# SwiGLU FFN of a decoder layer: gate and upper products by Strassen block sums, in two phases

## The chip, the core and the metric

The kernel runs on one core of a Trainium2 chip. The metric is the device time of one execution in microseconds (us); less is better. TensorE (PE) multiplies matrices, VectorE (DVE), ScalarE (ACT) and GpSimd (POOL) do elementwise work, SyncE (SP) issues DMAs. Each engine takes its instructions in the order of its own queue, and waits there for the engines or DMAs whose results it needs.

## The reference

One layer of a decoder: a combined projection, three head groups (a gated chunk MLP and two attentions), an output projection, and a SwiGLU FFN. D is 1024, D_FF is 2816; there are 1024 prompt tokens and 64 sample rows, 1088 in all. Everything is float32.

```python
def norm(x, g):                                    # rms_norm in the source
    y = x * rsqrt(mean(x * x, axis=-1) + EPS)
    return y * g
def swiglu(x, w_in, w_out):                        # w_in: 1024 x 5632, w_out: 2816 x 1024
    h = x @ w_in
    return (jax.nn.silu(h[..., :D_FF]) * h[..., D_FF:]) @ w_out
# one layer, for the prompt (1024 rows) and for the samples (8 x 8 rows, with a paged cache)
u, va, qb, kb, vb, qc, kc, vc, lf = split_proj(rms_norm(yp, g_attn) @ w_in, b_f)
a_out = chunk_spatial_gate(u, rms_norm(va, g_v), w_s, b_s)
b_out = sb_prompt(qb, kb, vb)                      # stick-breaking attention, 6 heads
c_out = fox_prompt(qc, kc, vc, lf)                 # forgetting attention, 6 heads
yp = yp + merge_groups(a_out, b_out, c_out, g_mix, w_o)
yp = yp + swiglu(rms_norm(yp, g_ffn), w_ffn_in, w_ffn_out)
y_prompt = rms_norm(yp, g_final)
```

## The kernel before

The change is in the FFN, which is the end of the program. A float32 product is formed from three products of operands in the fp32r type: each operand is split into a high part (an ACT copy) and a low part (the rest, a DVE subtraction), and high x high, high x low and low x high are added up in the same PSUM bank (lines 1326 to 1328).

Ahead of the FFN, `merge` adds the output projection to `y`, one tile of 128 tokens and one half of 512 columns after the other (`prod`, L1147 to L1153; its weights `wor`, `woh`, `wol`). `step` (L1247) normalises a token tile that is complete (`norm`, `xs` at L196) and, `LAG` = 4 tiles later, transposes an earlier one on PE (`spread`, L204) and writes its high part by ACT (`xh`, L206) and its low part by DVE (`xl`, L207). When the merge is done the last four tiles are still to be spread; L1317 to L1319 do that between the first and the second chunk of tokens of the first pair.

`y` stays in SBUF for the whole FFN, as do `xh2` and `xl2`, the two parts of all tokens. The FFN goes over 22 pairs of column blocks: block `ff` of the gate and block `ff` of the upper matrix, 1024 x 128 each. Each is loaded (`fraw_`, L1308), split (`fh`, `fl`, L1311 and L1312), and multiplied by three chunks of tokens (384, 384, 320), with 8 steps along D (L1325). ACT takes the Silu of the gate, DVE multiplies it by the upper (L1332), ACT and POOL split the result g (`g_h` L1333, `g_l` L1335). After every `FCH` = 2 pairs the output product runs: 9 token tiles x 2 halves of 512 columns, three matmuls per block and tile (`fout`, L1359 to L1362; two for the samples' tile), added to `y` by DVE (L1363). After the last group each tile is normalised and written out (`final`, L1281).

PSUM has two sets of banks: `fgu` shares three (set a), `fout` and `spread` share five (set b). The order on each engine is made by a scheduler when the program is built; a matmul waits for a bank until its last reader is done. SP issues the DMAs in one queue, first in, first out.

## Time and profile before

| | us |
|---|---|
| median of 3 runs (lowest, highest) | 1645.32 (1643.71, 1648.43) |
| the profiled execution | 1652.82 |
| its span | 1651.1 |
| PE busy in it | 1559.6 |
| DVE, ACT, POOL busy | 862.3, 627.7, 474.7 |
| mean granted clock of TensorE, share of full speed | 0.976 |

A profile belongs to one execution. A matmul's shown duration is longer than the distance to the next one's start, since matmuls are pipelined; what a matmul costs in a row of them is read from the distance of the starts. In the names, `fgu<-xh,fh` is a matmul from `xh` (moving) and `fh` (weights) into the PSUM tile `fgu`; 128x384 is partitions by columns of the moving operand.

### The profile page before, as it was taken

To read this page: it belongs to the slowest core of one execution; us is meant where nothing else is said; L and a number is where in the kernel's file an instruction comes from. 1 tells how busy PE (TensorE), PEld (TensorE's weight loads), DVE (VectorE), ACT (ScalarE), POOL (GpSimd) and SP (SyncE) were. 2 spreads that over 40 slices of the span, in tenths; PEclk is the share of its full clock that TensorE was granted. 3 is DMA by queue.
4 is the path that set the end of the run, shared out by engine and by line. 5 is a ranking of instruction groups with operands and counts; after the bars stand their busy time and mean duration, and the time that the engine had idled before them with its cause. 6 is when DMAs were issued, how large, how long until landed. Compare 5 with 4: busy or idle time off the path is not lost.

```text
span 1651.1 us, 23878 instructions
## 1 busy us (share of the span) xinstructions
PE 1559.6 (94%) x8980; PEld 1439.6 (87%) x8980; DVE 862.3 (52%) x1565; ACT 627.7 (38%) x1291; POOL 474.7 (29%) x596
## 2 busy tenths in 40 slices
...
GB/s 174 56 168 180 187 187 147 114 134 236 222 204 227 234 182 165 290 175 127 88 83 84 39 38 52 44 45 41 52 52 26 52 51 42 36 52 51 26 1 108
DMA packets 137303, 184.54 MB, mean 112 GB/s; under 512 B 17844, under 2 KB 110372, under 8 KB 137188
## 3 DMA queue, kind: packets, MB, share of 16 engines
...
## 4 chain that ended last, share of the span: by engine, by line
PE 52%; DVE 2%; DMA 2%; issue 1%; POOL 0%; ACT 0%; SPq 0%; DVEq 0%; POOLq 0%; ACTq 0%
PE fgu L1326 11%; PE fgu L1328 11%; PE fgu L1327 11%; PE fout L1360 5%; PE fout L1359 5%; PE fout L1362 5%; PE prod L1147 1%; PE prod L1148 1%; DMA lr<-linv 1%; PE prod L1150 1%; DMA wor<-in_w_o_dram 0%; DVE fl L1294 0%; PE spread L204 0%; DVE vh L812 0%; DVE cr L1107 0%
## 5 line engine op out<-in xcount | busy, mean ns | idle before, releaser
L1328 PE MATMUL fgu<-xh,fl 128*128 128x384 f32 (+1 forms) x1056 | 345.9, 328 | 1.0 <-DVE fl L1312 1.0
L1326 PE MATMUL fgu<-xh,fh 128*128 128x384 f32 (+1 forms) x1056 | 345.4, 328 | 0.8 <-ACT xh L206 0.5
L1327 PE MATMUL fgu<-xl,fh 128*128 128x384 f32 (+1 forms) x1056 | 345.7, 327 | 0.0
L1335 POOL TENSOR_TENSOR g_l<-sl,g_h 128x384 fp32r<-128x384 f32 (+1 forms) x66 | 75.1, 1138 | 672.9 <-ACT g_h L1333 672.9
L1363 DVE TENSOR_TENSOR y<-fout,y 128x512 f32<-128x512 f32 x198 | 135.6, 690 | 127.9 <-PE fout L1362 115.9
L1326 PEld LDWEIGHTS fgu<-xh,fh 128*128 128x128 f32 x1056 | 198.1, 188 | 2.9 <-ACT xh L206 0.8
L1328 PEld LDWEIGHTS fgu<-xh,fl 128*128 128x128 f32 x1056 | 198.3, 188 | 2.2 <-DVE fl L1312 1.3
L1327 PEld LDWEIGHTS fgu<-xl,fh 128*128 128x128 f32 x1056 | 198.3, 188 | 0.7
L1332 DVE TENSOR_TENSOR sl<-fgu,sl 128x384 f32<-128x384 f32 (+1 forms) x66 | 35.3, 535 | 301.4 <-PE fgu L1328 301.4
L1360 PE MATMUL fout<-fol,g_h 128*128 128x512 f32 x396 | 156.6, 395 | 0.0
L1359 PE MATMUL fout<-foh,g_h 128*128 128x512 f32 x396 | 156.5, 395 | 0.0
L1362 PE MATMUL fout<-foh,g_l 128*128 128x512 f32 x352 | 139.1, 395 | 0.0
L812 POOL TENSOR_TENSOR vh<-vr,vh 128x384 fp32r<-128x384 f32 x96 | 102.4, 1083 | 80.0 <-ACT vh L811 59.7
L1333 ACT CAST g_h<-sl 128x384 fp32r<-128x384 f32 (+1 forms) x66 | 32.6, 493 | 184.6 <-DVE sl L1332 184.6
L743 PE MATMUL sqk<-kt,qz 128*128 128x512 f32 x288 | 99.3, 439 | 3.0 <-DVE ats L800 1.2
L286 PE MATMUL pqk<-xh,wh 128*128 128x384 f32 (+1 forms) x288 | 97.0, 337 | 1.2 <-DVE pvt L599 0.6
L287 PE MATMUL pqk<-xl,wh 128*128 128x384 f32 (+1 forms) x288 | 95.5, 333 | 0.0
L288 PE MATMUL pqk<-xh,wl 128*128 128x384 f32 (+1 forms) x288 | 94.8, 333 | 0.0
L1360 PEld LDWEIGHTS fout<-fol,g_h 128*128 128x128 f32 x396 | 74.3, 188 | 16.7
L1359 PEld LDWEIGHTS fout<-foh,g_h 128*128 128x128 f32 x396 | 74.3, 188 | 16.7
L582 PE MATMUL apv<-at,vv 128*128 128x256 f32 x432 | 76.2, 299 | 10.3 <-DVE hl L302 4.8
L572 DVE TENSOR_TENSOR at<-atr,at 128x512 fp32r<-128x512 f32 (+2 forms) x144 | 76.3, 543 | 16.1 <-ACT at L571 15.5
...
## 6 DMA issues: line engine op xcount, KB each, us to landing
...
```

The source lines that it names most:

```text
L286: T.matmul(pm[:, 0:n], lhsT=wh, rhs=xh[:, k, o], start=k == 0, stop=False)
L287: T.matmul(pm[:, 0:n], lhsT=wh, rhs=xl[:, k, o], start=False, stop=False)
L288: T.matmul(pm[:, 0:n], lhsT=wl, rhs=xh[:, k, o], start=False, stop=k == KT - 1)
L743: T.matmul(pz, lhsT=queries(p, a, si), rhs=kts[t][p][:, b], start=si == 0 and p == 0 and n_ == 0, stop=si == 1 and p == 2 and n_ == 2)
L812: (V if t >= 16 and j in VL else G).tensor_tensor(vh[:, 1], vrs[t][:, j], f(vh[:, 0]), op=OP.subtract)
L1326: T.matmul(pm[:, 0:n], lhsT=h_[:, k], rhs=xh2[:, k, o], start=k == 0, stop=False)
L1327: T.matmul(pm[:, 0:n], lhsT=h_[:, k], rhs=xl2[:, k, o], start=False, stop=False)
L1328: T.matmul(pm[:, 0:n], lhsT=l_[:, k], rhs=xh2[:, k, o], start=False, stop=k == KT - 1)
L1359: T.matmul(pm, lhsT=gh[q][:, o], rhs=wh2[q][:, hs], start=q == 0, stop=False)
L1360: T.matmul(pm, lhsT=gh[q][:, o], rhs=wl2[q][:, hs], start=False, stop=i == 8 and end)
L1362: T.matmul(pm, lhsT=gl[q][:, o], rhs=wh2[q][:, hs], start=False, stop=end)
L1363: V.tensor_tensor(y[:, i, hs], pm, y[:, i, hs], op=OP.add)
```

## The change

The FFN becomes two phases. In the first the gate and upper products of all 22 pairs are made and g is written to DRAM (`gs`); in the second g and the weights of the output product are read back, split, and multiplied. `y` is written to DRAM (`ysc`) ahead of the first phase and read back (`z0` to `z7`) ahead of the second. In the first phase the tokens stand in two halves of 544 (`HT`), each in chunks of 272, and D in two halves, as `XH[d half, token half]` and `XL`.

Pairs 0 and 1 are multiplied in the ordinary form (`ordinary`), 192 matmuls of 272 columns each. The pairs from `NO` = 2 on take the 2 x 2 block product (gate and upper by token halves, over the two halves of D) in Strassen's form after Winograd: seven products instead of eight, of sums of blocks. The four sums of the tokens are made once, while the ordinary pairs run (`sums_of_tokens`, `last_sum`). The four sums of the weights are made for each pair on POOL (`wsum`), all seven weight blocks are split (`split`), and the seven products are put together by DVE, POOL and ACT (`first`, `second`). Products 1, 2, 3 of the next pair go before products 6, 5, 7, 4 of this one; the first three use the bank set a (`fgu`), the others set b (`fgs`).

In the second phase block 0 forms a group by itself, with operands made near the end of the first phase (`ops0`), and the other 21 blocks form seven groups of three (`FCH` = 3).

```diff
-FCH = 2
+FCH = 3
+HT = NTOK // 2
+RAWB, WSB = 2, 8
+NO = 2
+         "fgu": "a", "fgs": "b", "spread": "b", ...
+    gs = [dr.tile([128, NTOK], F32, name=f"gs{j}") for j in range(NFF)]
+    ysc = [dr.tile([128, D], F32, name=f"ysc{i}") for i in range(8)]
...
+    XH, XL = {}, {}
+    for th, dh in ((0, 0), (0, 1), (1, 1), (1, 0)):
+        XH[dh, th] = fp.tile([128, 4, HT], F32R, name=f"xh{dh}{th}")
+        XL[dh, th] = fp.tile([128, 4, HT], F32R, name=f"xl{dh}{th}")
...
+            if i < 8:
+                S.dma_start(ysc[i], y[i])
-            spread(x2, rows(i), i, xh2, xl2)
+            spread_halves(x2, rows(i), i)
     for _ in mg:
         step(LAG)
     ends[0](xin)
-    whole(8)
     pmp.close()
+    while xn:
+        step(0)
+    pyy.close()
...
+    def wload(j):
+        raws[j] = []
+        for half in range(2):
+            c0 = half * DFF + j * 128
+            r = slot(half)
+            if half:
+                r = f(r)[:, 0:D].rearrange("p (k c) -> p k c", c=128)
+            S.dma_start(r, w_ffn_in[0, :, c0:c0 + 128].rearrange("(k p) c -> p k c", p=128))
+            raws[j].append(r)
+    def wsum(j):
+        ga_, up = raws[j]
+        g1, g2, u1, u2 = ga_[:, 0:4], ga_[:, 4:8], up[:, 0:4], up[:, 4:8]
+        s1, s2, s3, s4 = (wf.tile([128, 4, 128], F32, name=f"s{x}") for x in range(4))
+        G.tensor_tensor(s1, u1, u2, op=OP.add)
+        G.tensor_tensor(s2, s1, g1, op=OP.subtract)
+        G.tensor_tensor(s4, g2, s2, op=OP.subtract)
+        G.tensor_tensor(s3, g1, u1, op=OP.subtract)
+        sums[j] = {1: g1, 2: g2, 3: s4, 4: u2, 5: s1, 6: s2, 7: s3}
+    def split(j, q):
+        src = sums[j].pop(q)
+        x = wf.tile([128, 2, 4, 128], F32R, name="ws", bufs=WSB)
+        A.copy(x[:, 0], src)
+        V.tensor_tensor(x[:, 1], src, f(x[:, 0]), op=OP.subtract)
+        parts[j, q] = x
+    NP = ((0, HT // 2), (HT // 2, HT))
+    FIRST, SECOND = (1, 2, 3), (6, 5, 7, 4)
+    XB = {}
+    def product(j, q, c):
+        a, b = NP[c]
+        w, (hi, lo) = parts[j, q], XB[q]
+        pm = bank([128, 512], "fgu" if q in FIRST else "fgs")
+        for k in range(4):
+            T.matmul(pm[:, 0:b - a], lhsT=w[:, 0, k], rhs=hi[:, k, a:b], start=k == 0, stop=False)
+            T.matmul(pm[:, 0:b - a], lhsT=w[:, 0, k], rhs=lo[:, k, a:b], start=False, stop=False)
+            T.matmul(pm[:, 0:b - a], lhsT=w[:, 1, k], rhs=hi[:, k, a:b], start=False, stop=k == 3)
+        return pm[:, 0:b - a]
+    def temp(name, bufs):
+        return wf.tile([128, HT // 2], F32, name=name, bufs=bufs)
+    def first(j, q, c):
+        pm = product(j, q, c)
+        a, b = NP[c]
+        if q == 1:
+            if c == 0:
+                gts[j, 0] = wf.tile([128, HT], F32, name="ga", bufs=2)
+            p = held[j, c, 1] = temp("p1", 4)
+            A.copy(p, pm)
+        elif q == 2:
+            o = gts[j, 0][:, a:b]
+            V.tensor_tensor(o, pm, held[j, c, 1], op=OP.add)
+            A.activation(o, o, AF.Silu)
+        else:
+            p = held[j, c, 3] = temp("p3", 4)
+            A.copy(p, pm)
+    def second(j, q, c):
+        pm = product(j, q, c)
+        a, b = NP[c]
+        if q == 6:
+            u = held[j, c, "u2"] = temp("u2", 2)
+            V.tensor_tensor(u, pm, held.pop((j, c, 1)), op=OP.add)
+        elif q == 5:
+            t = temp("t", 3)
+            V.tensor_tensor(t, pm, held[j, c, "u2"], op=OP.add)
+            if c == 0:
+                gts[j, 1] = wf.tile([128, HT], F32, name="gb", bufs=1)
+            o = gts[j, 1][:, a:b]
+            G.tensor_tensor(o, t, held.pop((j, c, 3)), op=OP.add)
+            A.activation(o, o, AF.Silu)
+            held[j, c, 5] = pm
+        elif q == 7:
+            u = held[j, c, "u3"] = temp("u3", 2)
+            V.tensor_tensor(u, pm, held.pop((j, c, "u2")), op=OP.add)
+            t = temp("t", 3)
+            V.tensor_tensor(t, held.pop((j, c, 5)), u, op=OP.add)
+            o = gts[j, 1][:, a:b]
+            G.tensor_tensor(o, o, t, op=OP.mult)
+            if c == 1:
+                S.dma_start(gs[j][:, HT:], gts.pop((j, 1)))
+        else:
+            t = temp("t", 3)
+            V.tensor_tensor(t, pm, held.pop((j, c, "u3")), op=OP.add)
+            o = gts[j, 0][:, a:b]
+            G.tensor_tensor(o, o, t, op=OP.mult)
+            if c == 1:
+                S.dma_start(gs[j][:, 0:HT], gts.pop((j, 0)))
+    XB[1], XB[2], XB[3] = ((XH[x], XL[x]) for x in ((0, 0), (1, 0), (1, 1)))
...
+    def ordinary(j, th, c):
+        a, b = NP[c]
+        pms = []
+        for h in range(2):
+            pm = bank([128, 512], "fgu")
+            for dh in range(2):
+                w, hi, lo = parts[j, (h, dh)], XH[dh, th], XL[dh, th]
+                for k in range(4):
+                    T.matmul(pm[:, 0:b - a], lhsT=w[:, 0, k], rhs=hi[:, k, a:b], start=dh == 0 and k == 0, stop=False)
+                    T.matmul(pm[:, 0:b - a], lhsT=w[:, 0, k], rhs=lo[:, k, a:b], start=False, stop=False)
+                    T.matmul(pm[:, 0:b - a], lhsT=w[:, 1, k], rhs=hi[:, k, a:b], start=False, stop=dh == 1 and k == 3)
+            pms.append(pm[:, 0:b - a])
+        if c == 0:
+            gts[j, th] = wf.tile([128, HT], F32, name="ga", bufs=2)
+        o = gts[j, th][:, a:b]
+        A.activation(o, pms[0], AF.Silu)
+        V.tensor_tensor(o, pms[1], o, op=OP.mult)
+        if c == 1:
+            S.dma_start(gs[j][:, th * HT:th * HT + HT], gts.pop((j, th)))
+    def sums_of_tokens(c):
+        a, b = NP[c]
+        for k in range(4):
+            (h11, l11), (h12, l12), (h21, l21), (h22, l22) = (
+                (f(XH[x][:, k, a:b]), f(XL[x][:, k, a:b])) for x in ((0, 0), (0, 1), (1, 0), (1, 1)))
+            t1, t2, t4 = temp("p1", 4), temp("p3", 4), temp("t", 3)
+            V.tensor_tensor(t1, h12, h11, op=OP.subtract)
+            V.tensor_tensor(t1, t1, l12, op=OP.add)
+            V.tensor_tensor(t1, t1, l11, op=OP.subtract)
+            V.tensor_tensor(t2, h22, t1, op=OP.subtract)
+            V.tensor_tensor(t2, t2, l22, op=OP.add)
+            G.tensor_tensor(t4, h21, t2, op=OP.subtract)
+            G.tensor_tensor(t4, t4, l21, op=OP.add)
+            for q, t, e in ((6, t2, V), (5, t1, V), (4, t4, G)):
+                hi, lo = (x[:, k, a:b] for x in XB[q])
+                A.copy(hi, t)
+                e.tensor_tensor(lo, t, f(hi), op=OP.subtract)
+    def last_sum(c):
+        a, b = NP[c]
+        for k in range(4):
+            h22, l22 = f(XH[1, 1][:, k, a:b]), f(XL[1, 1][:, k, a:b])
+            hi, lo = XH[0, 1][:, k, a:b], XL[0, 1][:, k, a:b]
+            t3 = temp(("u2", "u3")[k % 2], 2)
+            V.tensor_tensor(t3, h22, f(hi), op=OP.subtract)
+            V.tensor_tensor(t3, t3, l22, op=OP.add)
+            V.tensor_tensor(t3, t3, f(lo), op=OP.subtract)
+            A.copy(hi, t3)
+            V.tensor_tensor(lo, t3, f(hi), op=OP.subtract)
+    wload(0)
+    quarters(0)
+    wload(1)
+    ordinary(0, 0, 0)
+    if xn:
+        step(0)
+    ordinary(0, 0, 1)
+    whole(8)
+    while whole_ or xn:
+        step(0)
+    pxin.close()
+    ft = pool(pfp, "ft", side="left")
+    for q in (6, 5, 4):
+        XB[q] = (ft.tile([128, 4, HT], F32R, name=f"th{q}"), ft.tile([128, 4, HT], F32R, name=f"tl{q}"))
+    XB[7] = (XH[0, 1], XL[0, 1])
+    quarters(1)
+    wload(2)
+    ordinary(0, 1, 0)
+    sums_of_tokens(0)
+    ordinary(0, 1, 1)
+    wload(3)
+    for th, c in ((0, 0), (0, 1)):
+        ordinary(1, th, c)
+    sums_of_tokens(1)
+    wsum(NO)
+    for q in FIRST:
+        split(NO, q)
+    for c in range(2):
+        ordinary(1, 1, c)
+    last_sum(0)
+    for c in range(2):
+        for q in FIRST:
+            first(NO, q, c)
+    last_sum(1)
+    for q in SECOND:
+        split(NO, q)
+    wsum(NO + 1)
+    for q in FIRST:
+        split(NO + 1, q)
+    wload(NO + 2)
+    for j in range(NO, NFF):
+        if j + 1 < NFF:
+            for q in FIRST:
+                for c in range(2):
+                    first(j + 1, q, c)
+            for q in SECOND:
+                split(j + 1, q)
+        if j + 2 < NFF:
+            wsum(j + 2)
+        for q in SECOND:
+            for c in range(2):
+                second(j, q, c)
+        del raws[j]
+        if j + 2 < NFF:
+            for q in FIRST:
+                split(j + 2, q)
+        if j + 3 < NFF:
+            wload(j + 3)
+        if j == NFF - 2:
+            graw, raw, g_h0 = f(slot(1))[:, 0:NTOK], slot(0).rearrange("p k c -> p (k c)"), slot(1)
+            S.dma_start(raw, w_ffn_out[0, 0:128, :])
+            S.dma_start(graw, gs[0])
+            h_, l_, g_l0 = (wf.tile([128, 2, 4, 128], F32R, name="ws", bufs=WSB).rearrange("p a k c -> p (a k c)")
+                            for _ in range(3))
+            A.copy(h_, raw)
+            V.tensor_tensor(l_, raw, f(h_), op=OP.subtract)
+            A.copy(g_h0[:, 0:NTOK], graw)
+            G.tensor_tensor(g_h0[:, NTOK:], graw[:, SP_:], f(g_h0[:, SP_:NTOK]), op=OP.subtract)
+            V.tensor_tensor(g_l0, graw[:, 0:SP_], f(g_h0[:, 0:SP_]), op=OP.subtract)
+            ops0 = (g_h0, g_l0, h_, l_)
...
+    for i in range(8):
+        S.dma_start(y[i], ysc[i])
...
+    def out_operands(ff):
+        po = fo2[(ff - 1) // FCH % 2]
+        raw = fo.tile([128, D], F32, name="wor2", bufs=3)
+        S.dma_start(raw, w_ffn_out[0, ff * 128:ff * 128 + 128, :])
+        graw = fo.tile([128, NTOK], F32, name="gr", bufs=3)
+        S.dma_start(graw, gs[ff])
+        h_ = po.tile([128, D], F32R, name="foh", bufs=FCH)
+        l_ = po.tile([128, D], F32R, name="fol", bufs=FCH)
+        A.copy(h_, raw)
+        (G if ff == 2 else V).tensor_tensor(l_, raw, f(h_), op=OP.subtract)
+        g_h = po.tile([128, NTOK + NS], F32R, name="g_h", bufs=FCH)
+        g_l = po.tile([128, SP_], F32R, name="g_l", bufs=FCH)
+        A.copy(g_h[:, 0:NTOK], graw)
+        G.tensor_tensor(g_h[:, NTOK:], graw[:, SP_:], f(g_h[:, SP_:NTOK]), op=OP.subtract)
+        (V if ff % 2 and ff > 3 else G).tensor_tensor(g_l, graw[:, 0:SP_], f(g_h[:, 0:SP_]), op=OP.subtract)
+        made[ff] = (g_h, g_l, h_, l_)
...
+    for f0, nf in [(0, 1)] + [(x, FCH) for x in range(1, NFF, FCH)]:
+        for ff in range(f0 or 1, f0 + nf if f0 > 1 else 1 + FCH if f0 == 0 else 1):
+            out_operands(ff)
...
+        gh, gl, wh2, wl2 = zip(*(made.pop(ff) for ff in range(f0, f0 + nf)))
         for i in (8, 0, 1, 2, 3, 4, 5, 6, 7):
```

**The order on DVE at the first weight split.** Before: `xl` is a low part of the tokens, `xs` a normalised tile, `fl` at L1312 the low part of the first weight block.

```order
L196 SCALAR_TENSOR_TENSOR xs_9742<-y,rs,gfb 128x1024
L1138 TENSOR_TENSOR wol<-wor,woh 128x512 x2
L1089 TENSOR_SCALAR rv<-stat 128x1
L207 TENSOR_TENSOR xl_9285<-spread,xh_9284 128x4x128
L137 TENSOR_SCALAR ss<-ss 128x1
L207 TENSOR_TENSOR xl_9285<-spread,xh_9284 128x4x128
L1312 TENSOR_TENSOR fl<-fraw__9928,fh 128x1024
L1153 SCALAR_TENSOR_TENSOR y<-prod,fraw,y 128x512
L207 TENSOR_TENSOR xl_9285<-spread,xh_9284 128x4x128
```

After: `ws` at L1330 is the low part of the first weight block; `p` and `u` at L1436 and L1454 are sums of tokens in the making.

```order
L1454 TENSOR_TENSOR u_10727<-xh_9329,xh_9331 128x272
L1270 TENSOR_TENSOR xl_9332<-spread,xh_9331 128x4x128
L1270 TENSOR_TENSOR xl_9330<-spread,xh_9329 128x4x128
L1436 TENSOR_TENSOR p_10295<-p_10295,xl_9332 128x272
L1436 TENSOR_TENSOR p_10311<-p_10311,xl_9332 128x272
L1436 TENSOR_TENSOR p_10327<-p_10327,xl_9332 128x272
L140 TENSOR_SCALAR ss<-ss 64x1
L1436 TENSOR_TENSOR p_10343<-p_10343,xl_9332 128x272
L1330 TENSOR_TENSOR ws<-raw_10065,ws 128x512
```

The first split stood between two low parts of the tokens, with twelve more to come behind it; it now stands behind all spreads of the prompt's tiles and the first twelve operations of the sums.

**The order on DVE while the first pair is multiplied.** Before: `sl` at L1332 reads the PSUM bank of a chunk; it stands among the splits of weights.

```order
L1312 TENSOR_TENSOR fl<-fraw__10227,fh 128x1024
L1332 TENSOR_TENSOR sl<-fgu,sl 128x320
L1312 TENSOR_TENSOR fl<-fraw__10547,fh 128x1024
L1332 TENSOR_TENSOR sl<-fgu,sl 128x384 x2
L1312 TENSOR_TENSOR fl<-fraw__10553,fh 128x1024
L1332 TENSOR_TENSOR sl<-fgu,sl 128x320
```

After: `ga` at L1424 is the operation that reads the bank; `p`, `tl` are sums of tokens.

```order
L1424 TENSOR_TENSOR ga<-fgu,ga 128x272
L1439 TENSOR_TENSOR p_10296<-p_10296,xl_9330 128x272
L1439 TENSOR_TENSOR p_10312<-p_10312,xl_9330 128x272
L1439 TENSOR_TENSOR p_10328<-p_10328,xl_9330 128x272
L1439 TENSOR_TENSOR p_10344<-p_10344,xl_9330 128x272
L1424 TENSOR_TENSOR ga<-fgu,ga 128x272
L1270 TENSOR_TENSOR xl_9332<-spread,xh_9331 128x4x64
L1270 TENSOR_TENSOR xl_9330<-spread,xh_9329 128x4x64
L1445 TENSOR_TENSOR tl_10221<-p_10296,th_10220 128x272
```

The operation that frees a bank stood among splits of weights; it now stands among the sums of the tokens.

**The order in SP's queue where the second group of output operands is loaded.** Before, at the last two pairs: `fraw_` are weights, `out_dram` the results.

```order
L1308 DMA fraw__15156<-in_w_ffn_in_dram 128x8x128
L1308 DMA fraw__15162<-in_w_ffn_in_dram 128x8x128
L1345 DMA fraw__15336<-in_w_ffn_out_dram 128x1024
L1308 DMA fraw__15342<-in_w_ffn_in_dram 128x8x128
L1308 DMA fraw__15348<-in_w_ffn_in_dram 128x8x128
L1345 DMA fraw__15522<-in_w_ffn_out_dram 128x1024
L1296 DMA out_dram<-fh 64x1024
L1296 DMA out_dram<-fl 128x1024
```

After, at the passage between the phases: `z` is `y` read back, `gs_118` is g of the last pair, `wor` and `gr` are the operands of blocks 1 and 2.

```order
L1537 DMA z_15933<-ysc_122 128x1024
L1390 DMA gs_118<-gb 128x544
L1537 DMA z_15934<-ysc_123 128x1024
L1537 DMA z_15935<-ysc_124 128x1024
L1537 DMA z_15936<-ysc_125 128x1024
L1537 DMA z_15937<-ysc_126 128x1024
L1397 DMA gs_118<-ga 128x544
L1545 DMA wor_15949<-in_w_ffn_out_dram 128x1024
L1547 DMA gr<-gs_98 128x1088
L1545 DMA wor_15962<-in_w_ffn_out_dram 128x1024
L1547 DMA gr<-gs_99 128x1088
```

The loads for the output product stood among those of the gate and upper weights; they now stand in a row behind the writes of the last pair's g, with the reads of `y` between.

## Rows read from the trace of the kernel before

**Rows 1.** the page: busy time of each engine, and the chain that ended last

```profile
PE 1559.6 (94%) x8980; PEld 1439.6 (87%) x8980; DVE 862.3 (52%) x1565; ACT 627.7 (38%) x1291; POOL 474.7 (29%) x596
...
PE fgu L1326 11%; PE fgu L1328 11%; PE fgu L1327 11%; PE fout L1360 5%; PE fout L1359 5%; PE fout L1362 5%; PE prod L1147 1%; PE prod L1148 1%; DMA lr<-linv 1%; PE prod L1150 1%; DMA wor<-in_w_o_dram 0%; DVE fl L1294 0%; PE spread L204 0%; DVE vh L812 0%; DVE cr L1107 0%
```

**Rows 2.** windows: length, PE, PEld, DVE, ACT, POOL, PEclk, DMA, GB/s

```profile
1000.00:1100.00 100.00, 100.00 (x565) 95.23 (x564) 27.35 (x36) 16.92 (x27) 12.18 (x13) 1.00 0.17 51
```

**Rows 3.** timeline of PE: start us, us, operation, [idle before and its releaser]

```profile
60.08 0.28 PE L332 MATMUL ptok<-wh,xh 128*128 128x256 f32 x1
...
63.99 0.29 PE L332 MATMUL ptok<-wh,xh 128*128 128x256 f32 x1
...
402.87 1.97 PE L708 MATMUL str<-ct,kr 128*128 128x128 f32 x8 [6.16 <-DMA kr<-in_cache_fox_k_dram,idx]
...
1010.47 0.31 PE L1326 MATMUL fgu<-xh,fh 128*128 128x320 f32 x1
...
1017.51 0.34 PE L1326 MATMUL fgu<-xh,fh 128*128 128x384 f32 x1
...
1025.83 0.34 PE L1326 MATMUL fgu<-xh,fh 128*128 128x384 f32 x1
...
1638.45 0.40 PE L1362 MATMUL fout<-foh,g_l 128*128 128x512 f32 x1
```

**Rows 4.** groups by line and form: busy us, mean ns, idle before

```profile
L1328 PE MATMUL fgu<-xh,fl 128*128 128x384 f32 x704 | 237.1, 337 | 1.0 <-DVE fl L1312 1.0
...
L1328 PE MATMUL fgu<-xh,fl 128*128 128x320 f32 x352 | 108.8, 309 | 0.0
...
L1326 PEld LDWEIGHTS fgu<-xh,fh 128*128 128x128 f32 x1056 | 198.1, 188 | 2.9 <-ACT xh L206 0.8
```

**Rows 5.** windows, tile fgu alone: PE, PEld, DVE, ACT, PEclk, DMA, GB/s

```profile
841.50:864.00 22.50, 16.39 (x85) 14.58 (x86) 0.55 (x1) 0.49 (x1) 1.00 0.31 94
...
1000.00:1645.00 645.00, 424.35 (x2558) 421.23 (x2556) 28.92 (x54) 24.87 (x53) 1.00 0.15 45
```

**Rows 6.** timeline of DVE at the start of the FFN

```profile
839.41 1.27 DVE L196 SCALAR_TENSOR_TENSOR xs<-y,rs,gfb 128x1024 f32<-128x1024 f32 x1
840.61 1.28 DVE L1138 TENSOR_TENSOR wol<-wor,woh 128x512 fp32r<-128x512 f32 x2
...
842.54 0.68 DVE L207 TENSOR_TENSOR xl<-spread,xh 128x512 fp32r<-128x512 f32 x1
843.14 1.21 DVE L1312 TENSOR_TENSOR fl<-fraw__9928,fh 128x1024 fp32r<-128x1024 f32 x1
844.27 0.74 DVE L1153 SCALAR_TENSOR_TENSOR y<-prod,fraw,y 128x512 f32<-128x512 f32 x1
844.93 0.68 DVE L207 TENSOR_TENSOR xl<-spread,xh 128x512 fp32r<-128x512 f32 x1
```

**Rows 7.** groups of DVE by form, 500 to 1000 us

```profile
L599 DVE TENSOR_TENSOR pvt<-apv,pvt 64x256 f32<-64x256 f32 x20 | 8.1, 407 | 0.1
```

**Rows 8.** window behind a wait of PE, columns as in rows 2

```profile
402.90:407.40 4.50, 4.50 (x20) 4.40 (x20) 3.67 (x6) 2.54 (x5) 3.89 (x7) 0.50 1.02 406
```

**Rows 9.** groups of POOL by form

```profile
L1335 POOL TENSOR_TENSOR g_l<-sl,g_h 128x384 fp32r<-128x384 f32 x44 | 45.2, 1028 | 537.1 <-ACT g_h L1333 537.1
...
L558 POOL TENSOR_TENSOR at_g<-at_g,at_s 128x512 f32<-128x512 f32 x6 | 6.6, 1092 | 3.1 <-DVE at_s L556 2.8
```

**Rows 10.** timeline of DVE, then of POOL, at the tail

```profile
1636.31 1.27 DVE L1294 SCALAR_TENSOR_TENSOR fl<-y,rs,gfin 128x1024 f32<-128x1024 f32 x1
...
1638.10 3.29 DVE L1294 SCALAR_TENSOR_TENSOR fl<-y,rs,gfin 128x1024 f32<-128x1024 f32 x1
...
1637.95 2.36 POOL L1292 TENSOR_TENSOR fh<-fh,gfin 128x1024 f32<-128x1024 f32 x1
```

**Rows 11.** window with many transfers, columns as in rows 2

```profile
850.00:852.00 2.00, 2.00 (x13) 2.00 (x12) 2.00 (x2) 1.99 (x4) 0.00 (x0) 1.00 0.84 247
```

**Rows 12.** windows, tile fout alone: PE, PEld, DVE, PEclk, DMA, GB/s

```profile
1000.00:1645.00 645.00, 222.47 (x936) 175.02 (x936) 110.85 (x162) 1.00 0.15 45
```

134 lines of the change are left out of this document (57 added, 77 removed).

## The prediction

> **What bounds the kernel now.** I read first the page's busy times and chain of waits. TensorE (PE) is busy 94% of the span, and its three gate/up lines (L1326 to L1328) and three output lines (L1359 to L1362) are the head of the chain, with no other engine near them [rows 1]. Then the stretches: from 1000 to 1100 us PE is busy for all 100 us at the full clock, while DVE works 27, ACT 17 and POOL 12 us, and DMA uses 0.17 of its engines [rows 2]. So in the FFN a microsecond less of PE streaming is a microsecond less of time, as long as the other three can follow. The FFN runs from about 841.5 us to the last matmul at 1638.45 [rows 3].
>
> All durations are of one profiled execution of 1652.8 us (span 1651.1), 7.5 us above the median of the runs, 1645.3. I add the changes to 1652.8 and take the same difference off the median.
>
> **1. Fewer columns streamed: -56.8 us.** Before, a pair costs 8 k x 3 products x 2 halves x 3 chunks = 144 matmuls: 96 with 384 columns, 48 with 320. From start to start, 48 of 320 take 1010.47 to 1017.51, 146.7 ns each, and 48 of 384 take 1017.51 to 1025.83, 173.3 [rows 3]; all counted, lines x384 and x320 come three times each [rows 4], 2112 and 1056 matmuls, 520.9 us. The busy time of the tile in the stretch from 1000 to 1645 us is 424.35 us for 2558, 165.9 ns each, 525.6 us in all [rows 5]. I take 522.9, between them. After: pairs 0 and 1 have 192 matmuls of 272 columns, the other twenty 7 products x 2 chunks x 12 = 168, in all 3744. No row has 272 columns. A column costs (173.3 - 146.7)/64 = 0.416 ns, so 272 costs 126.7 by stepping down from 320; 33 matmuls of 256 columns take 60.08 to 63.99, 118.5 ns each [rows 3], stepping up 125.2; in proportion to 384 it is 122.8. I take 124.5: 466.1 us (459.8 to 474.4). The 1144 output matmuls stay as many and as wide, so they cost nothing new. 466.1 - 522.9 = -56.8, bounds -61 and -48.
>
> **2. The start of the FFN: +13.7 us.** Before, the first gate/up matmul starts after the spread of four token tiles, since `LAG` lets the rest follow the first chunk: 85 fall between 841.5 and 864 [rows 5]. After, PE has all spreads ahead of it and DVE has them ahead of the first weight split (`ws`, L1330). Up to 839.41 nothing differs. From there DVE does, by starts [rows 6]: 5 `xs` at 1.20; 4 `wol` splits at 0.60; 10 `xl` of 512 at 0.60 and four partial ones that make two more; 2 `y` at 0.66; the sample add, 1024 columns like an `xs`, at 1.20; 12 first sums of 272 columns at 0.35 (L599 with 256 columns shows 0.407 [rows 7], and starts lie some 0.07 closer than durations, 1.27 to 1.20 for the `xs`); 0.4 of small ones; the split 0.6. Together 23.5, and 0.9 for waits: 863.8. PE then has done 6 matmuls that need no low part where before had 85: 79 x 0.1733 = 13.7. Without waits 12.8; with each of the last four spreads late by one full `xs`, 18.
>
> That PE is idle for most of 842 to 864 has a second price. After a 6.16 us wait for a DMA at 402.87 [rows 3] the granted clock is 0.50 (1.2 GHz) for the next 4.5 us [rows 8], half of the work lost: **+2.3** (0 to 4.5).
>
> **3. The sums of the tokens under pairs 0 and 1: +10 us.** Between 863.8 and the first Strassen products PE has 378 matmuls x 0.1245 = 47 us. In it DVE has about 75 operations of 272 columns with both inputs in SBUF (26.3 us), 15 splits (9.0) and 16 products with the PSUM (6.7): 42. POOL has 24 operations of 272, by its 384-column row of 1.03 [rows 9] 0.73 each, 17.5, and 8 weight sums of 512 at 1.09: 26. Taken apart both fit. They are not apart: an SBUF operation of 1024 columns takes DVE 1.27 at 1636.31 and 3.29 at 1638.10, while POOL runs one of 2.36 [rows 10]. So 2.02 of POOL's 2.36 us were DVE's loss, 0.86. POOL's 26 us block 0.86 x 26 x 35/47 = 16 us of DVE, 6 of which fit into its free time: 10. Every chunk's PSUM bank is let go by a DVE product (L1424) that stands behind sums in DVE's queue, and three banks hold one chunk and a half, so PE waits for it. Ends: 2 (only the queue's ripple) and 20 (61 us of both in series, and the 6.7, less 47).
>
> The Trainium skill, in "SBUF — State Buffer", section "SBUF: two separate sides", calls the port pair of the two engines an exclusive lock that is held for the whole instruction. By that rule the sum takes the end of 20, not the 10; the row of 3.29 agrees with a full block of one operation, and no row here shows a long mixed stream.
>
> **4. The twenty pairs in steady state: 0.** PE has 168 x 0.1245 = 21 us per pair. DVE has 7 splits of 0.6, 14 product reads or adds of about 0.42 and a few more, 10 us; POOL 4 weight sums at 1.09 and 6 to 8 at 0.73, 9 to 10; ACT 7.5. Even with all of POOL's blocking DVE it is under 21. Banks are three for `fgu` and five for `fgs`; PE runs up to six blocks ahead of a DVE add, and I find over 2 us of slack at each release. The writes of g and loads of weights move 1.6 MB in 21 us, 76 GB/s, where a stretch of before carries 247 [rows 11].
>
> **5. Handoff between the phases: +9 us.** Let E be the end of the last Strassen product. SyncE's queue holds the reload of `z4`..`z7` behind the write of the last `gb` half (E - 1.3) and the operands of blocks 1 to 3 behind the last `ga` half (E + 1.4): 2.1 + 3.2 = 5.3 MB at 247 GB/s is 21.6 us, so block 3 lands at E + 23. ACT's cast (1.1) and POOL's low part follow, 1024 columns at 2.68 ns of its row [rows 9], 2.74: E + 27. PE has block 0 ready (52 matmuls, at the output tile's 222.47/936 = 0.238 [rows 12], 12.4 us) and 23 more before it needs that low part: E + 18. Loss 9. Low end 1, if the transfers cost nothing beyond POOL's own chain (first `gr` at E + 6, cast, four operations of 2.74: E + 18.4); high end 15, with the clock's 2.3 and POOL blocked by two splits. After it, a group of three has 156 matmuls x 0.238 = 37 us for 9 us of POOL: no wait.
>
> **6. The tail: -2 us.** The last group is three blocks wide, so a final norm (POOL 2.36, DVE 3.29 [rows 10]) has 4.3 us per output tile (2 halves x 9 x 0.238) where it had 2.9; the pile behind 1638.10 goes. Ends -4 and +1.
>
> **Sum:** -56.8 + 13.7 + 2.3 + 10 + 0 + 9 - 2 = -23.8. 1652.8 becomes 1629.0; off the median, 1621.5, say **1622**. With the terms' ends mostly independent the likeliest case spans 1612 to 1633.
>
> **The rivals.**
> (a) *The new waits are covered.* Sums lose 2, handoff 3: -56.8 + 13.7 + 2.3 + 2 + 3 - 2 = -37.8, 1608. For it: DVE and POOL use half of their time; against it: the row of 3.29.
> (b) *All start-up costs at their high ends.* Start 18, clock 4.5, sums 20, handoff 15: -56.8 + 57.5 - 2 = -1.3, 1644, no change. For it: the lock as a full block; against: four high ends at once.
> (c) *The other side: a bank wait in every pair.* POOL's four weight sums stand back to back, 4.4 us in which a split on DVE is blocked; behind the split stands the add that frees a bank of `fgu`. If that eats the slack and 2 us more, twenty pairs lose 40: -23.8 + 40 = +16, 1661. It decides from 24/20 = 1.2 us per pair and is slower than the noise from 1.4. Against it: three blocks of the other bank set (1.5 us each) lie between.
> (d) *A narrow matmul doesn't cost in proportion.* A weight load is 188 ns in the profile [rows 4] and is hidden under every matmul of 147 ns or more; were it to bound at 188, 3744 x 63.5 ns = 238 us more. 256 columns at 118.5 speak against it, though with weights of other lines. Break even is 130.8 ns per matmul; slower from 132.
>
> The Trainium skill ("TensorE: Matmul & The Clock Gate", section "LDWEIGHTS (loading the stationary operand)") puts a load of 128 columns at P/1.2, 107 ns, an estimate under 124.5; the row shows 188 from issue to end, and the 118.5 of 256 columns shows that 188 does not bind. By 107 term 1 stands.
>
> **How the numbers follow.** Likeliest 0.62, (a) 0.20, (b) 0.10, (c) 0.05, (d) 0.03. A measurement of this kernel tells 0.3%, 4.9 us, from no change. The range of 8 in 10 leaves out the lower half of (a) and most of (b), (c), (d): 1604 to 1642. Faster: the likeliest, (a) and half of (b): 0.88 with rounding. Same: the other part of (b), 0.06. Slower: most of (c) and (d), 0.06.
>
> **What would show it.** Starts of `fgu` and `fgs` matmuls 124 to 126 ns apart (1). The first low-part matmul at about 864, where before stood the 86th (2). Gaps on PE put down to DVE's L1424 between 864 and 925, 10 us in sum, with DVE operations of 272 columns well over 0.41 (3). PE at 100% from 930 on; a gap in each pair instead is (c). One gap of some 9 us after the last `fgs`, released by POOL (5). I am wrong if PE's cadence is over 130 ns, or if its idle time in the twenty pairs is over 20 us.

## The result, and the profile after

| | before | after |
|---|---|---|
| median (lowest, highest), us | 1644.51 (1640.28, 1648.43), 4 runs | 1616.18 (1614.39, 1618.62), 4 runs |
| ratio of the runs, 95% interval | | 0.9832 [0.9811, 0.9852] |
| profiled execution, its span | 1652.82, 1651.1 | 1616.61, 1614.6 |

The kernel is 28.3 us faster by the medians; -23.8 was forecast, and 1616.18 lies in the stated range. The two profiled executions differ by more, 36.2 us. A part of that is not the change's: the fourth normalised tile (`xs`) of the FFN starts at 839.41 us in the execution of before [rows 6] and, by the same place in DVE's order, here at 830.75. Up to there both kernels compute the same; the one thing that the change adds so early, against the prediction's "nothing differs", is the writes of `ysc`, which SyncE issues from 815.95.

```profile
830.75 1.27 DVE L201 SCALAR_TENSOR_TENSOR xs<-y,rs,gfb 128x1024 f32<-128x1024 f32 x1
...
853.66 0.68 DVE L1330 TENSOR_TENSOR ws<-raw,ws 128x512 fp32r<-128x512 f32 x1
```

In the thirteen executions profiled this start varied between 824 and 839 us (832.71 in e3 below, which is the kernel before but for 32 bytes of SBUF). So every trace below is measured from this point, the common point: from it to the end before takes 811.7 us, after 783.8, 27.9 less, which agrees with the medians.

PE's timeline after has few waits, in three places:

```profile
854.39 0.60 PE L1418 MATMUL fgu<-xh,ws 128*128 128x272 f32 x1 [1.52 <-DVE ws L1330]
...
884.87 0.59 PE L1416 MATMUL fgu<-xh,ws 128*128 128x272 f32 x1 [4.64 <-DVE ga L1424]
...
898.11 0.59 PE L1416 MATMUL fgu<-xh,ws 128*128 128x272 f32 x1 [5.51 <-ACT ga L1423]
...
1353.60 0.50 PE L1605 MATMUL fout<-foh,g_h 128*128 128x512 f32 x1 [2.09 <-POOL g_h L1555]
...
1358.31 0.96 PE L1606 MATMUL fout<-fol,g_h 128*128 128x512 f32 x3 [0.68 <-POOL fol L1551]
...
1361.90 0.50 PE L1608 MATMUL fout<-foh,g_l 128*128 128x512 f32 x1 [1.14 <-POOL g_l L1556]
...
1365.53 0.98 PE L1608 MATMUL fout<-foh,g_l 128*128 128x512 f32 x3 [0.34 <-POOL g_l L1556]
```

Windows of the same trace (length, busy time and count of PE, its weight loads (PEld), DVE, ACT, POOL, then granted clock, share of the DMA engines, GB/s):

```profile
850.60:857.40 6.80, 5.06 (x19) 4.42 (x20) 6.80 (x17) 4.82 (x8) 3.93 (x1) 0.50 0.06 16
...
884.90:888.60 3.70, 3.70 (x18) 3.70 (x19) 3.70 (x11) 2.90 (x8) 3.70 (x1) 0.57 0.00 0
898.20:901.40 3.20, 3.20 (x14) 3.20 (x15) 1.90 (x3) 0.90 (x3) 3.12 (x5) 0.50 0.01 3
901.40:1339.00 437.60, 437.60 (x3488) 437.60 (x3487) 235.54 (x400) 147.99 (x310) 202.05 (x199) 1.00 0.23 76
```

The last row is the steady state: PE without a gap for 437.6 us, 3488 matmuls, 125.46 ns each (between neighbouring starts of the `fgs` matmuls it is 125.4, which is used below). The first three are the starts behind a wait, at half clock (1.2 GHz), the second a little over it. The output tile alone, in a stretch of after and of the experiment e2 below (PE, PEld, DVE, clock, DMA, GB/s):

```profile
1370.00:1600.00 230.00, 230.00 (x1016) 190.47 (x1015) 80.00 (x118) 1.00 0.23 79
```

230.00/1016 is 226.4 ns per output matmul; in an unbroken row the starts are 226 or 227 ns apart, 227 in the sums below. Before, the last 104 output matmuls stand in such a row too; it begins with

```profile
1614.41 0.39 PE L1359 MATMUL fout<-foh,g_h 128*128 128x512 f32 x1
```

and ends with the one at 1638.45 [rows 3]: 24.04 us for 103 intervals, 233 ns each, 233.3 over all rows of them. The table puts the change together by the forecast's terms. Streaming is the count by the steady interval, before by the starts of [rows 3]: 520.9 us, where the forecast took 522.9. Waits are PE's gaps at the place. The start is what is left of the way from the common point once the other terms are taken off, in both kernels; so the sum has to come out, and is no test of the single rows.

| term, us | forecast | measured |
|---|---|---|
| 1 columns streamed: 3744 x 0.1254 less 520.9 | -56.8 | -51.4 |
| 2 start of the FFN | +13.7 | about +13.5 |
| half clock (41 matmuls, 0.1 each) | +2.3 | +4.1 |
| 3 waits under pairs 0 and 1 | +10 | +10.5 |
| 4 the twenty pairs | 0 | 0 |
| 5 passage between the phases (265.3 for 1143 x 0.227) | +9 | +5.8 |
| 6 tail: 12.7 after the last matmul's start, now 9.7 | -2 | -2.9 |
| output matmuls, 1144 x (0.227 - 0.2333) | 0 | -7.2 |
| sum | -23.8 | -27.6 of 27.9 |

### The profile page after: what moved, and what is told of

Read it like the earlier page. It is cut to its first block, busy times and chain, and to the rows that moved or that the text cites. A ratio compares the mean times of both kernels' runs of the same rounds, so it can differ in the third digit from the quotient of the medians.

```text
span 1614.6 us, 26341 instructions
## 1 busy us (share of the span) xinstructions
PE 1506.2 (93%) x9556; PEld 1389.8 (86%) x9556; DVE 1040.4 (64%) x1896; ACT 710.6 (44%) x1487; POOL 687.1 (43%) x767
## 4 chain that ended last, share of the span: by engine, by line
PE 74%; DMA 9%; DVE 8%; issue 3%; ACT 2%; POOL 2%; SPq 1%; DVEq 0%; POOLq 0%; ACTq 0%
PE fout L1606 5%; PE fout L1605 5%; PE fgs L1345 5%; PE fgs L1343 5%; PE fgs L1344 5%; PE fout L1608 5%; PE fgu L1345 4%; PE fgu L1343 4%; PE fgu L1344 4%; PE sqk L748 3%; PE pqk L291 3%; PE pqk L293 3%; PE pqk L292 3%; PE apv L587 2%; PE ptok L337 2%
## 5 line engine op out<-in xcount | busy, mean ns | idle before, releaser
L1609 DVE TENSOR_TENSOR z<-fout,z 128x512 f32<-128x512 f32 x128 | 86.6, 689 | 93.2 <-PE fout L1608 93.1
L1343 PE MATMUL fgu<-xh,ws 128*128 128x272 f32 x480 | 138.7, 289 | 0.0
L1343 PE MATMUL fgs<-th,ws 128*128 128x272 f32 x480 | 138.6, 289 | 0.0
L1345 PE MATMUL fgs<-th,ws 128*128 128x272 f32 x480 | 138.5, 289 | 0.0
L1345 PE MATMUL fgu<-xh,ws 128*128 128x272 f32 x480 | 138.5, 288 | 0.0
L1344 PE MATMUL fgu<-xl,ws 128*128 128x272 f32 x480 | 137.9, 287 | 0.0
L1344 PE MATMUL fgs<-tl,ws 128*128 128x272 f32 x480 | 137.9, 287 | 0.0
L1330 DVE TENSOR_TENSOR ws<-s,ws 128x512 fp32r<-128x512 f32 x80 | 74.6, 932 | 44.3 <-ACT ws L1329 41.7
L1330 DVE TENSOR_TENSOR ws<-raw,ws 128x512 fp32r<-128x512 f32 x68 | 58.6, 867 | 54.1 <-ACT ws L1329 54.1
L1344 PEld LDWEIGHTS fgs<-tl,ws 128*128 128x128 f32 x480 | 90.6, 189 | 0.0
L1344 PEld LDWEIGHTS fgu<-xl,ws 128*128 128x128 f32 x480 | 90.5, 189 | 0.0
L1343 PEld LDWEIGHTS fgs<-th,ws 128*128 128x128 f32 x480 | 90.4, 188 | 0.0
L1343 PEld LDWEIGHTS fgu<-xh,ws 128*128 128x128 f32 x480 | 90.3, 188 | 0.0
L1345 PEld LDWEIGHTS fgs<-th,ws 128*128 128x128 f32 x480 | 90.3, 188 | 0.0
```

The costliest lines, as they stand in the source:

```text
L1330: V.tensor_tensor(x[:, 1], src, f(x[:, 0]), op=OP.subtract)
L1343: T.matmul(pm[:, 0:b - a], lhsT=w[:, 0, k], rhs=hi[:, k, a:b], start=k == 0, stop=False)
L1344: T.matmul(pm[:, 0:b - a], lhsT=w[:, 0, k], rhs=lo[:, k, a:b], start=False, stop=False)
L1345: T.matmul(pm[:, 0:b - a], lhsT=w[:, 1, k], rhs=hi[:, k, a:b], start=False, stop=k == 3)
```

## The experiments

"Rest" is the time from the common point to the end in the profiled execution; after has 783.8. The next column is the part of it up to the start of the last gate or upper matmul; after has 508.7. In e1, e2, e6 and e8, whose first phase has the same matmuls as after's, it comes out within 0.5 us of that; smaller differences are not read from single traces.

| run | rest, us | first phase | rest against | median, us |
|---|---|---|---|---|
| e1 weights aligned | 783.5 | 508.8 | -0.3 to after | 1617.13 |
| e2 output misaligned | 791.0 | 508.9 | +7.1 to after | 1627.22 |
| e3 before aligned | 806.7 | (one phase) | -5.0 to before | 1639.44 |
| e7 two phases, ordinary | 832.3 | 554.2 | +48.5 to after | 1663.34 |
| e4 no sums of tokens | 771.8 | 493.0 | -12.1 to after | 1600.83 |
| e5 sums on DVE | 770.0 | 495.2 | -13.8 to after | 1602.54 |
| e9 three ordinary pairs | 780.9 | 506.2 | -3.0 to after | 1616.01 |
| e8 operands on ACT's queue | 782.2 | 509.2 | -1.7 to after | 1612.65 |
| e6 no operands ahead | 794.3 | 509.0 | +10.5 to after | 1626.86 |
| e10 = e5 and e8 | 767.0 | 495.8 | -16.8 to after | 1603.29 |
| e12 = e10, low part on DVE | 765.0 | 495.0 | -18.9 to after | 1598.13 |

**Why the output matmuls got faster.** In the built programs the two operands of an output matmul start 32 bytes apart in SBUF modulo 64 before, and agree after; the same 32 bytes stand between tokens and weights of the gate and upper matmuls in both. Two edits put a small tile beside a pool (e1 in after, e3 in before), one between the operands (e2).

```diff
+    pad = pool(wfst, "padp", side="right").tile([128, 8], F32, name="pad")   # e1, e3
+    G.memset(pad, 0.0)
     wf = pool(wfst, "wf", side="right")
...
+        if po not in padded:                                                 # e2
+            padded.append(po)
+            G.memset(po.tile([128, 8], F32, name="padg"), 0.0)
         g_h = po.tile([128, NTOK + NS], F32R, name="g_h", bufs=FCH)
```

> The changed kernel with 32 bytes put beside the pool of the first phase, so that the weights (ws) start at a multiple of 64 bytes, as the tokens do; before they stood 32 bytes off. Observation behind it: the 512-column output matmuls start 233.3 ns apart in the kernel before (tokens' g 32 bytes off from the moving weights) and 227 in the changed one (both at 0), and the output projection (both at 32) 227 in both. Theory A (the offset between the two operands costs about 7 ns per matmul at any width): 272 columns go from 125.4 to about 118.5 ns, 3744 of them, -26 us, 1590. Theory B (it costs only where 512 columns fill a bank): nothing, 1616. Theory C (the offset has nothing to do with it): nothing, 1616.

> The changed kernel with 32 bytes between the two operands of the output matmuls in both pools of the second phase, so that one starts at 0 and the other at 32 modulo 64 bytes, as in the kernel before; group 0 stays as it is. Theories A and B: 1092 matmuls go from 227 to 233-234 ns, +7.4 us, 1623 to 1624. Theory C (the cadence came from groups of three or from the phase without gate matmuls beside it): 227 stays, 1616.

> The kernel before with 32 bytes put beside its FFN pool, so that the operands of gate, upper and output matmuls agree modulo 64 bytes. Theory A: output 233.3 to 227 (1144 x 6.5 = -7.4 us) and 3168 gate and upper matmuls 7 ns less each (-22), about 1615. Theory B: only the output, -7.4, 1637. Theory C: nothing, 1644.5.

e2, the output tile in the same stretch as above:

```profile
1370.00:1600.00 230.00, 230.00 (x987) 185.22 (x987) 77.29 (x114) 1.00 0.22 76
```

987 where after has 1016 in 230 us: 233.0 ns. Apart from the one small fill of the inserted tile nothing but the distance of the addresses was changed, and the rest grew by 7.1 us, as theories A and B said (the median, 1627.22, grew by 11, more than their 1623 to 1624). e1 moved nothing: its steady state has the 3488 matmuls of after in the same 437.60 us.

```profile
903.20:1340.80 437.60, 437.60 (x3488) 437.60 (x3487) 235.40 (x400) 148.65 (x310) 201.91 (x199) 1.00 0.24 76
```

So A fell and B stands: of the widths tried here, the offset costs at 512 columns. e3, the output tile from 1000 to 1600 us, first in before, then in e3:

```profile
1000.00:1600.00 600.00, 198.04 (x832) 155.54 (x832) 98.82 (x144) 1.00 0.14 42
```

```profile
1000.00:1600.00 600.00, 194.45 (x832) 155.67 (x832) 98.86 (x144) 1.00 0.14 41
```

3.59 us less for 832 matmuls, 4.3 ns each, 4.9 us for all 1144; ratio to before 0.9957 [0.9937, 0.9978]. B had 6.5 each. The gate and upper matmuls stayed at 173.4 and 146.6 ns (384 and 320 columns), which A had 7 lower. In e3 the operands agree modulo 64 bytes but are 64 apart modulo 128, and intervals of 226 to 232 ns occur; in after they agree modulo 128 too. That this makes the missing 2 ns was not tried.

**What Strassen itself is worth.** e7 drives all pairs as the first two.

```diff
+    for j in range(NFF):
+        if j + 1 < NFF:
+            quarters(j + 1)
...
+                if j or th:
+                    ordinary(j, th, c)
```

> The changed kernel with all 22 pairs in the ordinary form and no sums of tokens or weights: two phases, quarter blocks, 272 columns, operands of block 0 ahead. My sum: 22 x 192 matmuls at 125.4 ns are 529.7 us where the changed kernel has 469.5, +60; the two waits of the sums (10.5) and their slow clock (1 to 2) go: +48, 1664, so slower than before by 20. Rival (the saving is in the two phases and the aligned output operands, Strassen pays only for its own waits): 1616 to 1630.

The rest is 48.5 us longer, and the ratio to before is 1.0105 [1.0055, 1.0155]: the two phases with their chunks of 272, without Strassen's form, are slower than before, by 18 us in the medians and 20.6 in the traces, and the form gives back 60 less its waits. The rival fell. Of the 48.5 the first phase has 45.5; the other 3 are from the passage, where PE stands in one piece

```profile
1400.26 0.79 PE L1568 MATMUL fout<-foh,g_h 128*128 128x512 f32 x1 [5.05 <-POOL g_h L1518]
```

and the eight output matmuls behind it start 427 ns apart, at a granted clock of 0.50. So the agreement with the expected 48 is closer than the sum behind it.

**The waits under the ordinary pairs.** In after, DVE, POOL and ACT around the two waits:

```profile
876.37 1.01 DVE L1435 TENSOR_TENSOR p<-xh,xh 128x272 f32<-128x272 f32 x1
...
884.39 0.42 DVE L1424 TENSOR_TENSOR ga<-fgu,ga 128x272 f32<-128x272 f32 x1
```

```profile
878.91 0.97 POOL L1440 TENSOR_TENSOR t<-xh,p 128x272 f32<-128x272 f32 x1
...
884.77 9.40 POOL L1445 TENSOR_TENSOR tl<-t,th 128x272 fp32r<-128x272 f32 x1 [3.07 <-ACT th L1444]
894.14 0.75 POOL L1440 TENSOR_TENSOR t<-xh,p 128x272 f32<-128x272 f32 x1
```

```profile
895.76 0.42 ACT L1444 CAST th<-t 128x272 fp32r<-128x272 f32 x1 [6.37 <-POOL t L1441]
...
897.66 0.40 ACT L1423 ACTIVATE ga<-fgu 128x272 f32<-128x272 f32 x1
```

Up to 882 us the two take turns: an operation of 0.42 on DVE takes about 1.0, one of 0.75 on POOL about 0.95. Then DVE runs its sums one behind the other, and POOL's next operation takes 9.40. ACT stands in front of a cast that waits for POOL, with the Silu (L1423) behind, and PE's bank waits for the Silu. e4 leaves the sums out, e5 gives POOL's share to DVE, e9 has three ordinary pairs.

```diff
-    def sums_of_tokens(c): ...                                  # e4: both empty,
-    def last_sum(c): ...                                        # XB[6], XB[5], XB[4] = XB[2], XB[1], XB[3]
...
-            G.tensor_tensor(t4, h21, t2, op=OP.subtract)        # e5
-            G.tensor_tensor(t4, t4, l21, op=OP.add)
+            V.tensor_tensor(t4, h21, t2, op=OP.subtract)
+            V.tensor_tensor(t4, t4, l21, op=OP.add)
-            for q, t, e in ((6, t2, V), (5, t1, V), (4, t4, G)):
+            for q, t, e in ((6, t2, V), (5, t1, V), (4, t4, V)):
...
-NO = 2
+NO = 3                                                          # e9, with quarters(2), ordinary(2, ...)
```

> The changed kernel without the sums of the tokens: products 6, 5 and 4 take the tokens' blocks 2, 1 and 3 in place of the sums, product 7 the block as it is, so the sums' work on DVE, POOL and ACT is left out and the result is another one. My term 3: the two waits of PE in the first pairs (4.64 and 5.51 us in the profile after) and the half clock behind them (about 2) go, and up to 3 at the start, where 12 sums stand ahead of the first split: 1600 to 1605. Rival (the waits are the form's own, by banks and the order of ACT's Silu): 1616.

> The changed kernel with the 24 token-sum operations of POOL moved to DVE; POOL keeps the sums of weights. Lock theory (two waits because DVE and POOL shut each other out: DVE sums at 0.93 us each beside POOL, and one POOL operation of 9.40 beside DVE, with ACT's Silu behind it): DVE does them at 0.35, has 50 us of work in 47, one wait of 3 to 5 stays: 1609 to 1612. Queue theory (waits come from the number of DVE operations ahead of the one that frees the bank): 24 x 0.35 = 8.4 more in the same queue, 1620 to 1624.

> The changed kernel with three pairs in the ordinary form in place of two, and the sums of tokens spread over them. One more ordinary pair costs 24 x 125.4 ns = 3.0 us. Lock theory: 61 us of DVE and POOL work then have 71 us of PE to hide under; the waits of 10.5 and about 2 of half clock go: 1606 to 1609. Queue theory (sums stand ahead of the freeing operation wherever they are): 1619.

e4 takes 12.1 us off, and both waits are gone; a window of 47 us in the first pairs:

```profile
846.00:893.00 47.00, 47.00 (x367) 46.78 (x367) 11.59 (x22) 9.69 (x20) 5.29 (x5) 0.97 0.25 75
```

That 12.1 is near the size of the waits is in part chance. The first phase is 15.7 shorter: 10.5 of waits, 2.9 at the start, and the rest clock. The passage takes 3.6 of it back, by a wait in one piece, with eleven output matmuls 427 ns apart behind it (granted clock 0.50):

```profile
1334.98 0.80 PE L1578 MATMUL fout<-foh,g_h 128*128 128x512 f32 x1 [4.59 <-POOL g_h L1528]
```

e5 takes off 13.8 with the sums still made, 13.5 of it in the first phase: the two waits and the clock behind them. Windows of 47 us, after and then e5 (columns as above):

```profile
856.00:903.00 47.00, 36.85 (x263) 36.20 (x263) 39.02 (x71) 13.24 (x35) 40.04 (x28) 0.88 0.23 69
```

```profile
858.00:905.00 47.00, 46.89 (x370) 46.46 (x370) 46.39 (x110) 17.77 (x45) 11.51 (x5) 0.99 0.25 75
```

DVE does 110 operations in the time in which it did 71, and PE 370 matmuls for 263. More work in DVE's queue made it shorter, so the queue theory fell. The lock theory had the sign, but gave only 4 to 7 us: it asked that all 50 us of DVE's work end under 47 us of PE, while the last sums may run on under the first Strassen products (in e5 five of their operations start behind the first of these, at 906.32). e5 does not by itself part the blocking from POOL being the slower engine for the same operation (0.75 against 0.42); the stretched operations in the trace of after, 1.01 and 9.40, show the blocking. e9 about halves the waits:

```profile
887.08 0.39 PE L1416 MATMUL fgu<-xh,ws 128*128 128x272 f32 x1 [2.08 <-DVE ga L1424]
...
895.39 0.39 PE L1416 MATMUL fgu<-xh,ws 128*128 128x272 f32 x1 [2.03 <-ACT ga L1423]
...
904.53 0.40 PE L1416 MATMUL fgu<-xh,ws 128*128 128x272 f32 x1 [1.15 <-DVE ga L1424]
```

It pays 3.0 for the third ordinary pair, and comes out 3.0 shorter in the trace but the same in its median, 1616.01, between the two theories' 1606 to 1609 and 1619: 24 us more of PE to hide under did not end the waits.

**The passage.** e8 issues three blocks' loads on ACT's queue, e6 takes the early operands of block 0 away, e12 also moves one low part.

```diff
-        S.dma_start(raw, w_ffn_out[0, ff * 128:ff * 128 + 128, :])
+        Q = A if ff <= FCH else S                               # e8; the same for graw
+        Q.dma_start(raw, w_ffn_out[0, ff * 128:ff * 128 + 128, :])
...
-            ops0 = (g_h0, g_l0, h_, l_)                         # e6
-        for ff in range(f0 or 1, ...):
+        for ff in range(f0, ...):
...
-        (G if ff == 2 else V).tensor_tensor(l_, raw, f(h_), op=OP.subtract)
+        V.tensor_tensor(l_, raw, f(h_), op=OP.subtract)         # e12, on e10
```

> The changed kernel with the loads of output operands 1 to 3 issued from ScalarE's queue instead of SyncE's, where they stand behind the writes of the last pair's g and the reads of y. My term 5: they land 6 to 10 us sooner and PE's five waits behind group 0 (5.8 us) go but for about 1: 1610 to 1612. Rival 1 (they wait for their tiles or for the DMA engines anyway): 1616. Rival 2 (ScalarE's queue is stopped by the issue, and its Silu with it): a wait in the last pairs, 1618 or more.

> The changed kernel without the operands of block 0 made ahead: all of blocks 0 to 3 are loaded and split at the passage, the first ring holds four blocks, and the weights' pool of the first phase is closed before it (the output tiles of the last norm have three buffers for four). My theory: PE then idles from the last Strassen product until block 0's operands are split, about 13 us, with 2 of half clock behind it, and blocks 1 to 3 come in under block 0's 12 us with 2 to 3 of waits, where the changed kernel waits 5.8: 9 to 12 us more, 1625 to 1628. Rival (making block 0 ahead only shifts the same wait behind its group): 1616 to 1618.

> The changed kernel with both earlier edits: all token sums on DVE, and the loads of output operands 1 to 3 issued from ScalarE's queue. If the two act in different places they add: from the common point before the FFN to the end the first took 13.8 us off, the second 1.7: 15.5, about 1600.5. If the second only worked because the first phase ended with another state of the queues: 1602.5, as with the first alone.

> As the one before, and the low part of block 2's output weights made by DVE instead of POOL. In the run with loads on ScalarE's queue PE's two waits at the passage, 1.05 and 0.76 us, are released by POOL, whose chain is four operations of 2.4 us. If POOL's chain is the limit, it is one operation shorter: 1 to 3 us less, about 1598.5. If the loads are the limit, no change against the run before; if DVE and POOL shut each other out there, 1 to 2 more.

The first cast of a loaded block in after, then in e8:

```profile
1350.29 1.05 ACT L1550 CAST foh<-wor 128x1024 fp32r<-128x1024 f32 x1 [14.77 <-DMA wor<-in_w_ffn_out_dram]
```

```profile
1343.14 1.05 ACT L1551 CAST foh<-wor 128x1024 fp32r<-128x1024 f32 x1 [11.65 <-DMA z<-ysc]
...
1347.97 2.37 POOL L1552 TENSOR_TENSOR fol<-wor,foh 128x1024 fp32r<-128x1024 f32 x1
```

The last Strassen matmul starts at 1339.41 in after and 1335.39 in e8, so the cast comes 10.9 us and 7.8 us behind it. That brought 1.7 us in the trace and not 4 to 6 (3.5 by the medians, whose ratios to before, 0.9815 [0.9778, 0.9852] and 0.9832, are not apart). Two rows of e8 bear on why it is less, first the transfers, then PE's clock:

```profile
1335.40:1347.00 11.60, 11.60 (x54) 9.63 (x53) 11.12 (x17) 3.57 (x4) 2.67 (x4) 1.00 1.01 391
...
1352.80:1355.80 3.00, 3.00 (x8) 2.31 (x7) 2.22 (x1) 1.99 (x2) 3.00 (x3) 0.50 0.50 152
```

The DMA engines are busy all the time, so the loads share them with the reads of `y`, and the first rival is likely right in part; and PE's next waits, 1.05 and 0.76, released by POOL, are followed by matmuls at half clock, which the passage of after did not have. The second rival fell: the first phase is as long as in after. e12, e10 with one of POOL's operations taken away, gets 2.0 more, and one wait of 0.44 remains:

```profile
1347.49 0.96 PE L1609 MATMUL fout<-foh,g_l 128*128 128x512 f32 x3 [0.44 <-POOL g_l L1557]
```

So both held back PE: first the loads, by their place in SyncE's queue (what the shared transfers add was not tried), then POOL's chain. In e6 PE stands from the last product to the first output matmul:

```profile
1353.02 0.80 PE L1593 MATMUL fout<-foh,g_h 128*128 128x512 f32 x1 [13.01 <-POOL g_h L1544]
```

10.5 us more than with block 0 ahead, so that part of the change earns its place. e10 adds up in the trace (16.8 where 15.5 was expected); its median, 1603.29, is no better than e5's 1602.54, so the runs' times do not show the second edit on top of the first. e12 is the best version: median 1598.13 (1594.48 to 1602.45), ratio to before 0.9711 [0.9674, 0.9747], where the change has 0.9832; from e10's 0.9739 [0.9702, 0.9776] the times alone do not part it.

## Why the prediction was right

1. *Columns.* Right in kind, 5.4 us short. 272 columns take 125.4 ns, where 124.5 was taken of 122.8 to 126.7: 3.4. The other 2.0 are in the 522.9, a middle between the time by starts, 520.9, and the busy time, 525.6; what a matmul costs in a row is read from the starts. e7's first phase has the price of the ordinary form: 60.2 more for the columns, 14.7 less for waits, clock and start. Rival (d), a floor by the weight loads, fell: they are still 188 to 189 ns long and hidden.
2. *Start.* The first matmul with a low part starts 23.6 us behind the common point; 24.4 was worked out from DVE's queue. e4, without the sums, has it 20.8 behind its common point (824.16), so twelve sums ahead of the split cost 2.9:

```profile
844.93 0.60 PE L1418 MATMUL fgu<-xh,ws 128*128 128x272 f32 x1
```

The clock was priced here alone, at 2.3; 13 of the 41 matmuls at half clock stand at the start, 1.3 us, and the other 28 behind the two waits of the sums, 2.8 us that the forecast had in no term.

3. *Sums.* The size was right (10.15 us idle for 10), the path half, so the close agreement is in part luck. The first wait is the one that was named: DVE's L1424 behind sums, stretched by POOL. The second came from the other direction: POOL shut out for 9.40 us by DVE, and ACT's queue behind POOL. The port rule of the Trainium skill ("SBUF — State Buffer", section "SBUF: two separate sides") speaks of an exclusive lock for a whole instruction; the turns of 1.01 and 0.97 agree with it. The forecast laid on it the end of 20 us, which did not come, since PE needed only part of that work in time: the last four of POOL's eight sums of weights start at 915.63, after 11.59 us without work on POOL and only just ahead of the first Strassen product at 917.91:

```profile
915.63 4.41 POOL L1320 TENSOR_TENSOR s<-raw 128x512 f32<-128x512 f32 x1 [11.59 <-DVE ws L1330]
```

Why POOL got no turn during its 9.40 us, no run here shows.

4. *Steady state.* Right: no gap of PE between 901.4 and 1339. DVE's splits of weight sums are stretched, as rival (c) had it, 932 ns where unhindered ones take 675, but the slack holds:

```profile
L1330 DVE TENSOR_TENSOR ws<-s,ws 128x512 fp32r<-128x512 f32 x80 | 74.6, 932 | 44.3 <-ACT ws L1329 41.7
```

5. *Passage.* Sign and cause right, 5.8 for 9. Errors offset each other. The first `gr` was there at E + 11.8, not E + 6, but the transfers ran at 367 GB/s, where [rows 11] gave 247, and POOL's low parts took 2.4, not 2.74; a window, then ACT and POOL:

```profile
1341.00:1351.00 10.00, 10.00 (x46) 8.29 (x45) 10.00 (x16) 0.71 (x1) 0.11 (x1) 1.00 0.97 367
...
1351.55 1.10 ACT L1554 CAST g_h<-gr 128x1088 fp32r<-128x1088 f32 x1 [0.22 <-DMA gr<-gs]
...
1363.07 2.40 POOL L1556 TENSOR_TENSOR g_l<-gr,g_h 128x1024 fp32r<-128x1024 f32 x1
```

So block 3's low part was ready at E + 25.8, 1.2 ahead of the forecast's E + 27 (E is 1339.7). The larger part is PE's: 36 matmuls of blocks 1 to 3 had started before its last wait, at 1365.53, where 23 were counted, 3.0 us.

6. *Tail.* Right: the last norms of DVE at full width take 1.28 each, where one had 3.29 [rows 10]:

```profile
1600.76 1.28 DVE L1585 SCALAR_TENSOR_TENSOR yo<-z,rs,gfin 128x1024 f32<-128x1024 f32 x1 [0.93 <-POOL rs L1577]
```

The step that failed is in term 1: "The 1144 output matmuls stay as many and as wide, so they cost nothing new." They gave 7.2 us, a quarter of the gain, by where the new pools put their operands. The trace at hand held the hint: at the prediction's own 0.416 ns a column, 512 columns step up from the 173.3 of 384 to 226.5 ns, and before they took 233.3. Against these 7.2 and the passage's 3.2 stand 5.4 of the columns and 1.8 of the clock, so the errors cancel for the larger part, by luck: 1622 for 1616. Some sums of the prediction are off by little and change nothing: the items of term 2 add up to 23.3, not 23.5; DVE's free time in term 3 is 5, not 6; the low end of term 5 is E + 18.1, not E + 18.4.
